# One decoder layer on one core: the key latent projected before the query latent, and the query latent's norm moved into the softmax

## The chip, the cores and the metric

The kernel runs on one core of one Trainium2 chip. The metric is the device time of one execution in microseconds. Engines are named as in the profile: PE (matrix multiply), PEld (its weight loads), DVE (VectorE), ACT (ScalarE), POOL (GpSimd), SP (SyncE, which issues most DMAs here).

## The reference, cut to what matters

The layer has 256 tokens, width 2048, and two attention groups of 8 heads that share one input projection. Group A is a dilated sliding-window attention. Group B is a multi-head latent attention: a 512-wide query latent and a 512-wide key/value latent are normalised, and projected up again to heads.

```python
a_q, a_k, a_v, c_q, c_kv, k_r = split(rmsnorm(x) @ w_in)
...                                        # group A
c_q = _rmsnorm(c_q, q_latent_norm)         # x * rsqrt(mean(x*x) + eps) * gain
q_b = c_q @ w_uq                           # 8 heads x (128 plain + 64 rotary)
q_rope = _rope(q_rope, positions)
c_kv = _rmsnorm(c_kv, kv_latent_norm)
kv = c_kv @ w_ukv                          # 8 heads x (128 key + 128 value)
k_rope = _rope(k_r, positions)             # one rotary key for all heads
b_out = softmax(causal(q_full @ k_full.T * (128 + 64) ** -0.5)) @ v_b
x = x + rmsnorm(concat(a_out, b_out) @ w_out)
x = x + rmsnorm(relu(rmsnorm(x) @ w_up) ** 2 @ w_down)
```

The query latent's reciprocal root mean square is one number for each token, and everything from the latent to the scores (projection, rotary, product with keys) is linear in it. It may therefore be multiplied in at the latent or at the scores of that query.

## The kernel before, in words

Every fp32 matrix product is done in three passes: each operand is split into a rounded part `hi` (ScalarE) and a rest `lo` (VectorE), and PE adds hi*hi, hi*lo and lo*hi in PSUM (`split`, line 310, and `split_gain`, line 316, which multiplies a gain in). Weights come by SP's DMA into five raw buffers (`Weights.load`, line 192), and are split into eight hi and eight lo buffers, six tiles ahead of their use (`Weights.emit` and `get`, lines 200 and 229). The order of the weight tiles is the order in which chunks are planned: lines 328 to 343. A tile is split only when the tile eight places earlier is used up.

The program is written out in one order for all engines, and every engine takes its own instructions of it in that order. A planner, `Flow` (line 135), decides the order while the program is traced. PE's projections are the main line and move a clock by the planner's own costs (`MM`, line 131, for a matmul of 512 columns; `TR`, line 132, for a transpose). Side work is written as generators ("chains") which yield a delay. After every few matmuls `pump` runs each chain whose time has come; `finish` runs chains until the named ones are done. The delays stand in lines 89 to 98. The clock is the planner's and not the chip's: where an engine is later than the planner thought, the engines behind it wait.

PSUM has eight banks. Four hold projections in turn (`acc_bank`, line 292), two hold transposes (`tp_bank`, line 295), two hold scores and attention outputs (`at_bank`, line 298). A group that takes a bank waits until the last reader of its former content is done.

The stretch around the change, after group A's projections:

- `proj` (line 463) of cq (line 749), then of ckv with the rotary key (line 752); ScalarE copies the results to SBUF, scaled by the first norm's rstd. Meanwhile group A's last four heads run as two chains (`heads_a`, line 653).
- `latent` (line 726) is a chain for each latent: ScalarE squares, VectorE and POOL make the rstd (`rstd_of`, line 499), VectorE multiplies it in (line 734), PE transposes in two groups (`cqt`, `ckvt`), and ScalarE and VectorE split each group into the transposed hi and lo with the latent's gain. The query's lies beside the ckv projection, the key's is started after it (line 776), and must be finished before k0 (line 851).
- `shared_key` (line 762): rotary on the 64 shared key columns, twice for the two halves of the partitions, two transposes (`krt`), two copies.
- The loop over `B_ORDER` (line 836): qr (rotary parts of all query heads), q0 and q1 (plain query heads 0 to 3 and 4 to 7), k0 and k1, v0 and v1. `columns` (line 785) makes heads with channels on partitions and asks for both weight tiles of its chunk at its start; `proj` makes tokens on partitions, and asks for one at a time. After qr the chain `query_ropes` (line 803) rotates and transposes (`qrt`).
- After k0, three workers (`heads_b`, line 817) take the heads w, w+3, w+6, started `D_PAIR` apart. Each waits, asking again every 0.5, until the chains of the rotary query and rotary key are gone and its keys are made; then scores (`sc_b`), softmax, transposes (`pT_b`), output (`o_b`), split into `mixT`.
- The output projection (`acc_o`) begins after v1, on group A's heads, and the last heads of B run among its matmuls.

Of the kernel before, what the change touches and what calls it, by code (L numbers as in the profile page):

```python
# [18 lines left out]
F32 = mybir.dt.float32  # L19
F32R = mybir.dt.float32r  # L20
I32 = mybir.dt.int32
BF16 = mybir.dt.bfloat16
AF = mybir.ActivationFunctionType
OP = mybir.AluOpType
PSUM = bass.MemoryType.PSUM

P = 128
D = 2048
S = 256
NB = S // P  # L30
KD = D // P
HA = 8
HB = 8
NOPE = 128
RB = 64
RA = 32
QR = 512
KVR = 512
# [5 lines left out]
SCALE_A = 128.0 ** -0.5  # L44
SCALE_B = float((NOPE + RB)) ** -0.5
# [35 lines left out]
X_PIECES = ((2, 1, 1), (3, 2, 2), (5, 4, 3), (8, 7, 3), (11, 10, 3), (14, 13, 3))  # L81

N_WARM = 8
B_ORDER = ("qr", "q0", "k0", "v0", "q1", "k1", "v1")
N_WORK = 3
OUT_PIECES = ((0, 0, 512), (1, 0, 512), (2, 0, 512), (3, 0, 256), (3, 256, 256))


DA = (3.0, 0.5, 3.0, 3.0, 4.0, 3.0, 0.5)
DB = (1.0, 0.5, 2.0, 3.0, 3.0, 2.0)  # L90
D_PAIR, D_KR = 3.5, 2.0
D_LOADED, D_LATENT = (13.0, 9.0), 3.5
D_X0, D_X, D_SS, D_TAB = 8.0, 3.0, 3.0, (14.0, 20.0)
D_NORM, D_HT, D_SECOND = 4.5, 1.5, 4.0

# [175 lines left out]
def layer(nc, tc, io):  # L271
    flow = Flow()
# [51 lines left out]
    weights = Weights(nc, wp, split, W_BUFS, W_AHEAD)  # L324
# [3 lines left out]
    w_in, K2 = io["w_in"], [2] * (KD // 2)  # L328
    ch_a = {}
    for half in range(2):  # L330
        if not half:
            ch_a[0, "qk"] = TwoChunk(weights, w_in, (0, 1024))
        for i, nm in enumerate("qkv"):
            if half or nm == "v":
                ch_a[half, nm] = Chunk(weights, w_in, i * 1024 + half * 512, 512, K2)
    ch_cq = Chunk(weights, w_in, 3 * 1024, QR, K2)
    ch_ckv = Chunk(weights, w_in, 3 * 1024 + QR, KVR + RB, [1] * KD, [(0, 288), (288, 288)])
    ch_b = []
    for what in B_ORDER:
        first = {"q": 0, "k": 0, "v": HB * NOPE}[what[0]] + 512 * (2 if what == "qr" else int(what[1]))  # L340
# [105 lines left out]
    for c in range(2):  # L446
        wide_d.append([])
        for what, k in DOWN_STEPS[c]:
            if what == "k":
                ts = [weights.plan(down_weight(c, k), 1, CW)]  # L450
            else:
                q, parts_q, back = [lambda c=c, k=k, f=f: f(c, k) for f in (down_sums, down_split, down_back)]
# [57 lines left out]
    pa = pool("pa", "right")  # L510
    early = pool("early", "left")
    mixT = [mix.tile([P, HA + HB, S], F32R, name=f"mixT_{w}") for w in ("hi", "lo")]
    mix.tile([P, 64], F32, name="mix_pad")
    xT = [pa.tile([P, KD, S], F32R, name=f"xT_{w}") for w in ("hi", "lo")]
# [42 lines left out]
    freq, bias_a, bias_b = cst[:, 0:192], cst[:, 192:448], cst[:, 448:704]  # L557
# [4 lines left out]
    rstd0 = []  # L562
# [56 lines left out]

    def softmax_pv(wk, dl, sc, bias, scale, v, head, name, need=lambda: True):  # L620

        s = wk.tile([P, 384], F32, tag="s", bufs=2 if scale == SCALE_A else N_WORK, name=f"s_{name}")
        st = wk.tile([P, 8], F32, tag="st", bufs=3, name=f"st_{name}")
        spans = ((0, 128, bias[:, 128:256]), (128, 384, bias))
        for i, (a, e, m) in enumerate(spans):
            nc.vector.tensor_tensor_reduce(
                out=s[:, a:e], in0=sc[:, a:e], in1=m, op0=OP.add, op1=OP.max, scale=1.0,
                scalar=-3e38, accum_out=st[:, i:i + 1])
        nc.vector.tensor_scalar_mul(st[:, 2:4], st[:, 0:2], -scale)
        yield dl[2]  # L630
        for i, (a, e, m) in enumerate(spans):
            nc.scalar.activation(s[:, a:e], s[:, a:e], AF.Exp, bias=st[:, 2 + i:3 + i], scale=scale,
                                 accum_out=st[:, 4 + i:5 + i])
        yield dl[3]
        nc.vector.reciprocal(st[:, 6:8], st[:, 4:6])
        for i, (a, e, m) in enumerate(spans):
            nc.vector.tensor_scalar_mul(s[:, a:e], s[:, a:e], st[:, 6 + i:7 + i])
        yield dl[4]
        tp = tp_bank(f"pT_{name}")
        for c in range(3):  # L640
            transpose(tp[:, c * P:(c + 1) * P], s[:, c * P:(c + 1) * P])
        pT = wk.tile([P, 384], F32, tag="pT", bufs=2 if scale == SCALE_A else N_WORK, name=f"pT_{name}")
        nc.scalar.activation(pT, tp[:, :384], AF.Copy)
        yield dl[5]
        while not need():
            yield 0.5
        o = at_bank(f"o_{name}")
        mm(o[:, :S], v[0], pT[:, :S], True, False, 2 * MM)
        mm(o[:, P:S], v[1], pT[:, S:384], False, True, MM)
        split(mixT[0][:, head, :], mixT[1][:, head, :], o[:, :S])  # L650
# [48 lines left out]
    heads, evacs = [], []  # L699
    for half in range(2):  # L700
        qkv = {}
        for nms in (("qk", "v") if not half else "qkv"):
            accs = [acc for _, _, acc in proj(xT, [ch_a[half, nms]], f"{nms}{half}",
                                              bank_of=at_bank if (half, nms) == (0, "v") else None)]
            for i, nm in enumerate(nms):
                if half and nm == "v":
                    flow.finish(*heads)
                if not half and nm != "v":
                    t = early.tile([P, NB + 1, 512], F32, name=f"{nm}_{half}")
# [10 lines left out]
    lat = pool("lat", "left")  # L720
    ckv = lat.tile([P, NB, KVR + RB], F32, name="ckv")
    cq = lat.tile([P, NB, QR], F32, tag="cq", name="cq")
    ss1 = con.tile([P, 2, NB], F32, name="ss1")
    latT = {"q": [t[:, HA + 4:, :] for t in mixT]}

    def latent(c, i, n, pl):

        for b in range(NB):
            junk = pl.tile([P, 512], BF16, tag="junk", bufs=1, name=f"junk_{n}{b}")
            nc.scalar.activation(junk, c[:, b, :512], AF.Square, accum_out=ss1[:, i, b:b + 1])  # L730
        rstd = rstd_of(ss1[:, i, :], NB, 512, n)
        yield 1.5
        for b in range(NB):
            nc.vector.tensor_scalar_mul(c[:, b, :512], c[:, b, :512], rstd[:, b:b + 1])
        yield 1.0
        cT = latT[n]
        for k2 in range(2):
            t = tp_bank(f"c{n}t_{k2}")
            for kk in range(2):
                k = 2 * k2 + kk  # L740
                for b in range(NB):
                    transpose(t[:, kk * S + b * P:kk * S + (b + 1) * P], c[:, b, k * P:(k + 1) * P])
            for kk in range(2):
                k = 2 * k2 + kk
                g = (4 if n == "kv" else 0) + k
                split_gain(cT[0][:, k, :], cT[1][:, k, :], t[:, kk * S:(kk + 1) * S], gcol[:, g:g + 1])
            yield 1.0

    for _, b, acc in proj(xT, [ch_cq], "cq"):
        nc.scalar.activation(cq[:, b, :], acc[0], AF.Copy, scale=rstd0[0][:, b:b + 1])  # L750
    q_chain = flow.start(latent(cq, 1, "q", lat), D_LATENT)
    for _, b, acc in proj(xT, [ch_ckv], "ckv"):
        for i in range(2):
            nc.scalar.activation(ckv[:, b, i * 288:(i + 1) * 288], acc[i][:, :288], AF.Copy, scale=rstd0[0][:, b:b + 1])
    flow.finish(q_chain, *heads)
    pa.release()
    pb = pool("pb", "right")


    krT = pb.tile([P, 2, S], F32, name="krT")  # L760

    def shared_key():
        kr = pb.tile([P, NB, 2, RB], F32, name="kr")
# [7 lines left out]
        for j in range(2):  # L771
            nc.vector.tensor_copy(krT[j * 64:(j + 1) * 64, j, :], t[j * 64:(j + 1) * 64, :S])

    latT["kv"] = [pb.tile([P, 4, S], F32R, name=f"ckvT_{w}") for w in ("hi", "lo")]
    pb.tile([P, 104], F32, name="pb_pad")
    kv_chain = flow.start(latent(ckv, 0, "kv", lat), 2.0)
    kr_chain = flow.start(shared_key(), D_KR)

    kT = pb.tile([P, HB, S], F32, name="kT")
# [37 lines left out]
    def heads_b(hs):  # L817
        for h in hs:
            while any(c in flow.chains for c in (qr_chain, kr_chain)):
                yield 0.5  # L820
            while f"k{h // 4}" not in made:
                yield 0.5
            yield DB[0]
            sc = at_bank(f"sc_b{h}")
            for o, b in ((0, 0), (128, 1)):
                n = (b + 1) * P
                qs = slice(b * P, (b + 1) * P)
                mm(sc[:, o:o + n], qT[:, h, qs], kT[:, h, :n], True, False, (b + 1) * MM)
                mm(sc[:, o:o + n], qrT[:, h // 2, qs], krT[:, h % 2, :n], False, True, (b + 1) * MM)
            yield DB[1]  # L830
            yield from softmax_pv(pb, DB, sc, bias_b, SCALE_B, [vB[:, b, h, :] for b in range(NB)], HA + h, f"b{h}",
                                  lambda: f"v{h // 4}" in made)
            made.add(h)

    workers = []
    for what, ch in ch_b:
        if what in ("qr", "v0", "v1"):
            if what == "qr":
                qr = lat.tile([P, NB, HB, RB], F32, tag="cq", name="qr")
            for _, b, acc in proj(latT["q" if what == "qr" else "kv"], [ch], what):  # L840
                if what == "qr":
                    out = qr[:, b].rearrange("p h d -> p (h d)")
                else:
                    i = 4 * int(what[1])
                    out = vB[:, b, i:i + 4, :].rearrange("p h d -> p (h d)")
                nc.scalar.activation(out, acc[0], AF.Copy)
            if what == "qr":
                qr_chain = flow.start(query_ropes(qr), 1.0)
        else:
            if what == "k0":  # L850
                flow.finish(kv_chain)
            t, i = qT if what[0] == "q" else kT, 4 * int(what[1])
            for h2, acc in columns(latT["q" if what[0] == "q" else "kv"], ch, what):
                h = i + 2 * h2
                nc.scalar.activation(t[:, h:h + 2, :].rearrange("p h s -> p (h s)"), acc, AF.Copy)
        made.add(what)
        if what == "k0":
            workers = [flow.start(heads_b(range(w, HB, N_WORK)), w * D_PAIR) for w in range(N_WORK)]


# [571 lines left out]
```

## Time and profile before

| what | value |
|---|---|
| three timed runs | 1034.48, 1035.3, 1038.92 us (median 1035.3) |
| profiled execution, whole | 1032.79 us |
| its span | 1031.0 us |
| granted PE clock | 0.998 |
| busy in the span: PE, DVE, ACT, POOL | 99%, 81%, 61%, 7% |
| cq projection | 144 to 170 us of the span |
| ckv projection | 170 to 200 us |
| qr to v1 | 200 to 259 us |
| output projection, up, down | 259 to 353, 353 to 690, 690 to 1023 us |

The span is the profiler's, from first to last instruction; the profiled execution's own time lies 1.8 us above it. A row of the timeline has its start, its busy time, engine, line, operation, output from inputs, count, and in brackets the idle time before it with what ended it. The line of a matmul is always the helper's (L303), so its tile's name tells what it belongs to; L313 and L314 are the plain split, L317 and L318 the split with a gain.

### The profile page before, as it was taken

The page shows a single profiled execution, that of the slowest core. Times are in us where ns is not written, and L with a number is a line of the kernel's source. Part 1 is how long each engine was busy: PE and PEld are TensorE (multiplying, and loading weights), DVE is VectorE, ACT ScalarE, POOL GpSimd, SP SyncE. Part 2 cuts the span into 40 slices and gives each one's busy share as a digit, 9 for nine tenths or more (in the row PEclk, how much of TensorE's full clock was granted, in tenths as well). Part 3 has the DMA queues.
Part 4 walks back from the last instruction along what each step waited for, and adds up shares of the span by engine and source line. Part 5 has one row for each costly group of instructions (what it writes and reads, how often), then busy time and mean ns, then how long its engine had stood idle before and what let it go on. Part 6 is the DMA issues. An engine that isn't in the chain of part 4 may idle for free.

```text
span 1031.0 us, 13295 instructions
## 1 busy us (share of the span) xinstructions
PE 1016.5 (99%) x4726; PEld 847.8 (82%) x4726; DVE 833.2 (81%) x1109; ACT 629.9 (61%) x838; POOL 73.7 (7%) x116
## 2 busy tenths in 40 slices
PE   9999999989999999999999999999999999999996
PEld 6888888989888878888888888888888888888885
DVE  6777655665547579999999999898999999898896
ACT  6675544645545467666775767666666665767571
POOL 0020100000001000000100100000101000211100
PEclk9999999999999999999999999999999999999999
DMA  9987553743466478877989878589989877889972
GB/s 297 370 258 248 191 196 99 245 151 105 145 221 188 138 299 279 271 244 253 284 257 303 277 246 266 189 267 349 350 265 366 299 239 262 297 310 304 318 262 82
DMA packets 106035, 257.65 MB, mean 250 GB/s; under 512 B 8944, under 2 KB 27888, under 8 KB 105584
## 3 DMA queue, kind: packets, MB, share of 16 engines
q1 hardware_dynamic: 65200, 175.14, 50.9%
q0 software_dynamic: 17392, 61.87, 18.1%
q10 hardware_dynamic: 23376, 19.78, 6.0%
q8 instruction: 37, 0.61, 0.2%
q14 instruction: 30, 0.25, 0.1%
HBM read 226.88 MB, written 29.89 MB: 249 GB/s over the span
## 4 chain that ended last, share of the span: by engine, by line
PE 79%; DVE 2%; issue 1%; DMA 1%; ACT 1%; POOL 0%; DVEq 0%; POOLq 0%; ACTq 0%
PE acc_u L303 26%; PE y L303 25%; PE acc_o L303 8%; PE md L303 6%; PE m L303 6%; PE acc_ckv L303 2%; PE acc_k L303 1%; PE acc_v L303 1%; PE sc_b L303 1%; PE acc_q L303 1%; DMA raw<-in_w_uq 1%; PE y L1300 1%; DVE lo L318 0%; PE o_b L303 0%; PE pT_b L307 0%
## 5 line engine op out<-in xcount | busy, mean ns | idle before, releaser
L314 DVE TENSOR_TENSOR lo<-raw,hi 128x1024 fp32r<-128x1024 f32 (+2 forms) x205 | 233.0, 1159 | 81.9 <-ACT hi L313 81.0
L313 ACT ACTIVATE hi<-raw 128x1024 fp32r<-128x1024 f32 (+2 forms) x205 | 202.1, 1004 | 76.7 <-DMA raw<-in_w_in 20.9
L303 PE MATMUL acc_u<-hi,hT_lo 128*128 128x512 f32 x386 | 150.3, 389 | 0.4 <-DVE hT_lo L314 0.4
L303 PE MATMUL acc_u<-hi,hT_hi 128*128 128x512 f32 x386 | 150.7, 390 | 0.0
L303 PE MATMUL acc_u<-lo,hT_hi 128*128 128x512 f32 x386 | 150.2, 389 | 0.0
L303 PE MATMUL y<-hi,uhi 128*128 128x512 f32 x358 | 139.3, 389 | 0.0
L303 PE MATMUL y<-lo,uhi 128*128 128x512 f32 x358 | 139.3, 389 | 0.0
L303 PE MATMUL y<-hi,ulo 128*128 128x512 f32 x358 | 139.3, 389 | 0.0
L317 ACT ACTIVATE hi<-raw,gcol 128x1024 fp32r<-128x1024 f32 x86 | 97.1, 1149 | 35.9 <-DMA raw<-in_w_up 15.4
L318 DVE SCALAR_TENSOR_TENSOR lo<-raw,gcol,hi 128x1024 fp32r<-128x1024 f32 x86 | 106.9, 1274 | 9.8 <-ACT hi L317 9.8
L303 PEld LDWEIGHTS acc_u<-hi,hT_lo 128*128 128x128 f32 x386 | 72.5, 188 | 16.0 <-DVE hT_lo L314 0.9
L303 PEld LDWEIGHTS acc_u<-hi,hT_hi 128*128 128x128 f32 x386 | 72.5, 188 | 14.8
L303 PEld LDWEIGHTS acc_u<-lo,hT_hi 128*128 128x128 f32 x386 | 72.5, 188 | 14.7
L303 PEld LDWEIGHTS y<-lo,uhi 128*128 128x128 f32 x358 | 67.2, 188 | 14.1
L303 PEld LDWEIGHTS y<-hi,uhi 128*128 128x128 f32 x358 | 67.2, 188 | 13.9
L303 PEld LDWEIGHTS y<-hi,ulo 128*128 128x128 f32 x358 | 67.2, 188 | 13.9
L314 DVE TENSOR_TENSOR lo<-st_down,hi 128x1024 fp32r<-128x1024 f32 x46 | 55.0, 1219 | 0.6 <-ACT hi L313 0.6
L303 PE MATMUL acc_o<-hi,mixT_hi 128*128 128x512 f32 x128 | 50.5, 394 | 0.0
L313 ACT ACTIVATE hi<-u 128x1024 fp32r<-128x1024 f32 (+1 forms) x33 | 32.2, 979 | 29.9 <-PE acc_u L303 12.8
L313 ACT ACTIVATE hi<-st_down 128x1024 fp32r<-128x1024 f32 x46 | 47.7, 1048 | 3.8 <-DVE st_down L370 2.4
L303 PE MATMUL md<-hi,s 128*128 128x512 f32 x138 | 49.9, 389 | 0.0
L303 PE MATMUL acc_o<-hi,mixT_lo 128*128 128x512 f32 x128 | 49.9, 390 | 0.0
(348 smaller groups left out, 2030.0 us busy)
## 6 DMA issues: line engine op xcount, KB each, us to landing
raw<-in_w_up SPq DMA_DIRECT2D x86, 512.0 KB, 4.9
raw<-in_w_down SPq DMA_DIRECT2D x82, 512.0 KB, 5.9
raw<-in_w_in SPq DMA_DIRECT2D x55, 512.0 KB, 5.7
ab<-in_w_up POOLq DMA_DIRECT2D x17, 1024.0 KB, 6.8
raw<-in_w_out SPq DMA_DIRECT2D x32, 512.0 KB, 4.7
ab_down<-in_w_down POOLq DMA_DIRECT2D x11, 1024.0 KB, 9.6
ulo<-ukeep POOLq DMA_DIRECT2D x20, 512.0 KB, 6.8
rkeep<-r ACTq DMA_DIRECT2D x28, 256.0 KB, 3.3
```

The lines of the kernel that those rows point to most:

```text
L303: nc.tensor.matmul(out, a, b, start=start, stop=stop)
L313: nc.scalar.activation(hi, src, AF.Copy)
L314: nc.vector.tensor_tensor(out=lo, in0=src, in1=hi.bitcast(F32), op=OP.subtract)
L317: nc.scalar.activation(hi, src, AF.Copy, scale=g)
L318: nc.vector.scalar_tensor_tensor(out=lo, in0=src, scalar=g, in1=hi.bitcast(F32), op0=OP.mult, op1=OP.subtract)
L1300: nc.tensor.matmul(out, a[x], w[z], start=False, stop=(x, z) == (1, 0), skip_group_check=True)
```

## The change

The key latent is projected first and the query latent second. The query latent is no longer multiplied by its rstd; the rstd, times the softmax scale and its negative, is kept in a small tile `by_query`, and the softmax takes it as a scale by partition (a partition is a query there). The chunks come as k0, qr, q0, v0, k1, q1, v1; the key latent's transposes take the place in `mixT` that the query's had, and the other way round. The workers start after q0, and ask for queries as well as keys. Some of the planner's delays change.

```diff
-B_ORDER = ("qr", "q0", "k0", "v0", "q1", "k1", "v1")
+B_ORDER = ("k0", "qr", "q0", "v0", "k1", "q1", "v1")
-D_PAIR, D_KR = 3.5, 2.0
-D_LOADED, D_LATENT = (13.0, 9.0), 3.5
+D_PAIR, D_KR = 3.5, 6.0
+D_LOADED, D_LATENT = (13.0, 9.0), 3.0
...
+    ch_ckv = Chunk(weights, w_in, 3 * 1024 + QR, KVR + RB, [1] * KD, [(0, 288), (288, 288)])
     ch_cq = Chunk(weights, w_in, 3 * 1024, QR, K2)
-    ch_ckv = Chunk(weights, w_in, 3 * 1024 + QR, KVR + RB, [1] * KD, [(0, 288), (288, 288)])
...
-        nc.vector.tensor_scalar_mul(st[:, 2:4], st[:, 0:2], -scale)
+        if isinstance(scale, float):
+            scales = [scale] * 2
+            nc.vector.tensor_scalar_mul(st[:, 2:4], st[:, 0:2], -scale)
+        else:
+            scales = [scale[:, 0, b:b + 1] for b in range(NB)]
+            nc.vector.tensor_tensor(out=st[:, 2:4], in0=st[:, 0:2], in1=scale[:, 1, :], op=OP.mult)
...
-            nc.scalar.activation(s[:, a:e], s[:, a:e], AF.Exp, bias=st[:, 2 + i:3 + i], scale=scale,
+            nc.scalar.activation(s[:, a:e], s[:, a:e], AF.Exp, bias=st[:, 2 + i:3 + i], scale=scales[i],
...
-    latT = {"q": [t[:, HA + 4:, :] for t in mixT]}
+    latT = {"kv": [t[:, HA + 4:, :] for t in mixT]}
...
         rstd = rstd_of(ss1[:, i, :], NB, 512, n)
-        yield 1.5
-        for b in range(NB):
-            nc.vector.tensor_scalar_mul(c[:, b, :512], c[:, b, :512], rstd[:, b:b + 1])
-        yield 1.0
+        if n == "kv":
+            yield 2.0
+            for b in range(NB):
+                nc.vector.tensor_scalar_mul(c[:, b, :512], c[:, b, :512], rstd[:, b:b + 1])
+            yield 3.0
+        else:
+            for j, f in enumerate((SCALE_B, -SCALE_B)):
+                nc.vector.tensor_scalar_mul(by_query[:, j], rstd, f)
...
-    for _, b, acc in proj(xT, [ch_cq], "cq"):
-        nc.scalar.activation(cq[:, b, :], acc[0], AF.Copy, scale=rstd0[0][:, b:b + 1])
-    q_chain = flow.start(latent(cq, 1, "q", lat), D_LATENT)
     for _, b, acc in proj(xT, [ch_ckv], "ckv"):
...
-    flow.finish(q_chain, *heads)
+    kv_chain = flow.start(latent(ckv, 0, "kv", lat), D_LATENT)
+    for _, b, acc in proj(xT, [ch_cq], "cq"):
+        nc.scalar.activation(cq[:, b, :], acc[0], AF.Copy, scale=rstd0[0][:, b:b + 1])
+    flow.finish(kv_chain, *heads)
...
+    by_query = pb.tile([P, 2, NB], F32, name="by_query")
...
-    latT["kv"] = [pb.tile([P, 4, S], F32R, name=f"ckvT_{w}") for w in ("hi", "lo")]
+    latT["q"] = [pb.tile([P, 4, S], F32R, name=f"cqT_{w}") for w in ("hi", "lo")]
...
-    kv_chain = flow.start(latent(ckv, 0, "kv", lat), 2.0)
+    q_chain = flow.start(latent(cq, 1, "q", lat), 2.0)
...
-            while f"k{h // 4}" not in made:
+            while not {f"k{h // 4}", f"q{h // 4}"} <= made:
...
     for what, ch in ch_b:
+        if what == "qr":
+            flow.finish(q_chain)
...
-            if what == "k0":
-                flow.finish(kv_chain)
...
-        if what == "k0":
+        if what == "q0":
             workers = [flow.start(heads_b(range(w, HB, N_WORK)), w * D_PAIR) for w in range(N_WORK)]
```

More of the change, by code (lines that the diff above doesn't have):

```diff
@@ L620, in softmax_pv @@
     def softmax_pv(wk, dl, sc, bias, scale, v, head, name, need=lambda: True):
-        s = wk.tile([P, 384], F32, tag="s", bufs=2 if scale == SCALE_A else N_WORK, name=f"s_{name}")
+        s = wk.tile([P, 384], F32, tag="s", bufs=2 if wk is pa else N_WORK, name=f"s_{name}")
         st = wk.tile([P, 8], F32, tag="st", bufs=3, name=f"st_{name}")
@@ L641, in softmax_pv @@
             transpose(tp[:, c * P:(c + 1) * P], s[:, c * P:(c + 1) * P])
-        pT = wk.tile([P, 384], F32, tag="pT", bufs=2 if scale == SCALE_A else N_WORK, name=f"pT_{name}")
+        pT = wk.tile([P, 384], F32, tag="pT", bufs=2 if wk is pa else N_WORK, name=f"pT_{name}")
         nc.scalar.activation(pT, tp[:, :384], AF.Copy)
@@ L830, in heads_b @@
             yield DB[1]
-            yield from softmax_pv(pb, DB, sc, bias_b, SCALE_B, [vB[:, b, h, :] for b in range(NB)], HA + h, f"b{h}",
+            yield from softmax_pv(pb, DB, sc, bias_b, by_query, [vB[:, b, h, :] for b in range(NB)], HA + h, f"b{h}",
                                   lambda: f"v{h // 4}" in made)
```

## The prediction

> **What bounds the kernel now.** I began with the page's first part: the PE is busy for all but 14.5 us of the span, so an edit can take time away only where the PE stands still, or add it by making it stand still.
>
> ```profile
> span 1031.0 us, 13295 instructions
> PE 1016.5 (99%) x4726; PEld 847.8 (82%) x4726; DVE 833.2 (81%) x1109; ACT 629.9 (61%) x838; POOL 73.7 (7%) x116
> ```
>
> The table of waits, for the PE alone, then says where. Four of its waits lie in the stretch that the diff touches: for the transposes of the two latents (cqt, ckvt) and for one score.
>
> ```profile
> PE ckvt L307 <- DVE ckvT_lo L318: 2.6, 1, 2.6
> ...
> PE cqt L307 <- DVE mixT_lo L318: 1.1, 1, 1.1
> PE ckvt L307 <- DVE ckv L734: 0.5, 1, 0.5
> ...
> PE sc_b L303 <- DVE mixT_lo L314: 0.3, 1, 0.3
> ```
>
> The busy time by stretch (columns: PE, PEld, DVE, ACT, POOL, clock, DMA share, GB/s) agrees, and shows that what follows has no hole in the PE.
>
> ```profile
> 170.00:200.00 30.00, 28.86 (x215) 28.27 (x214) 20.29 (x37) 19.95 (x40) 0.72 (x1) 1.00 0.61 187
> 200.00:230.00 30.00, 26.95 (x178) 24.44 (x177) 21.30 (x41) 16.93 (x30) 1.17 (x2) 1.00 0.55 179
> ...
> 370.00:690.00 320.00, 320.00 (x1414) 265.05 (x1413) 295.26 (x341) 217.61 (x253) 20.22 (x26) 1.00 0.82 269
> ```
>
> A wait costs more than its idle time, because the end of a matmul is modelled. In the PE's timeline starts of ckv matmuls lie 0.13 apart, so the second cqt group came 181.59 - 180.22 - 0.13 = 1.24 late, 0.16 more than its 1.08.
>
> ```profile
> 180.22 0.29 PE L303 MATMUL acc_ckv<-hi,xT_lo 128*128 128x288 f32 x1
> 181.59 0.63 PE L307 MATMUL cqt<-ident,cq 128*128 128x128 f32 x4 [1.08 <-DVE mixT_lo L318]
> ...
> 265.55 1.47 PE L303 MATMUL o_b<-pT_b,vB 128*128 128x256 f32 x8
> 267.30 0.49 PE L303 MATMUL sc_b<-kT,qT 128*128 128x128 f32 x2 [0.28 <-DVE mixT_lo L314]
> ```
>
> With 0.16 added to each, the four waits cost 4.5 + 0.64 = 5.1 us. That is all there is to win here.
>
> **What goes.** The old order starts the key latent's chain when the PE has only qr and q0 left to run, and transposes the key latent, the shared key and the key latent again through two PSUM banks in turn; the third group waits for the bank of the first, which VectorE leaves late, having weight splits ahead. In the new order the key latent has the whole cq projection as cover. I followed the planner's clock by hand with its own costs (lines 89 to 98, 131, 132), first for the kernel before, where it gives the order of the trace, then for the diff. Between the two ckvt groups of the new order no other transpose is issued (both second heads of A have theirs before them), and between the two cqt groups neither, since the shared key is due at 6.0. So each pair takes both banks. The 1.1 + 2.6 + 0.5 go, and the score's 0.3 passes into the waits of third outputs, below. Gain 5.1. The two 128x512 scalings of cq also go from VectorE; they lay beside PE work and are worth nothing. The matmuls and weight bytes are the same, and SP still loads in the order of use; only the 16 ckv and 8 cq tiles, and the pairs of w_uq and w_ukv, change places.
>
> **What comes.** Prices of groups on the PE come from the chain of waits.
>
> ```profile
> 178.95 0.45 PE cqt L307 x4
> ...
> 212.28 4.31 PE acc_q L303 x36
> ...
> 225.29 1.31 PE sc_b L303 x8
> ...
> 232.10 1.31 PE sc_b L303 x8
> ...
> 237.00 0.33 PE pT_b L307 x3
> ...
> 248.40 2.07 PE acc_v L303 x9
> ...
> 255.52 0.65 PE o_b L303 x4
> ```
>
> First the query latent. Let the PE leave cq at time 0. It runs k0 (48 matmuls at 4.31/36 = 0.12, so 5.75) with both cqt groups among it (0.87), reaches qr at 6.6, and after 15 of its matmuls (0.23 each) the shared key's transposes at 10.0. Against it run these, from the timelines of the PE, ScalarE, VectorE and GpSimd:
>
> ```profile
> 238.59 0.28 PE L303 MATMUL acc_k<-ckvT_hi,hi 128*128 128x256 f32 x1
> 238.79 0.60 ACT L855 ACTIVATE qT<-acc_q 128x512 f32<-128x512 f32 x1 [0.78 <-PE acc_q L303]
> 239.29 2.00 ACT L313 ACTIVATE hi<-raw 128x1024 fp32r<-128x1024 f32 x2
> 240.37 2.36 DVE L314 TENSOR_TENSOR lo<-raw,hi 128x1024 fp32r<-128x1024 f32 x2 [2.28 <-ACT hi L313]
> ...
> 202.00 0.62 ACT L730 ACTIVATE junk_kv<-ckv 128x512 bf16<-128x512 f32 x1
> 203.28 0.19 ACT L730 ACTIVATION_READ_ACCUMULATOR junk_kv<-ckv 128x1 f32 x1
> 203.75 0.70 POOL L505 TENSOR_TENSOR rstd_kv<-t_kv,neg_half 128x2 f32<-128x2 f32 x1 [26.93 <-DVE t_kv L504]
> 203.61 0.29 DVE L615 TENSOR_TENSOR rp_kr<-ckv,trig 128x128 f32<-128x128 f32 x1
> 205.31 0.29 DVE L618 TENSOR_TENSOR kr<-rp_kr,rp_kr 128x128 f32<-128x128 f32 x1
> 210.51 0.47 ACT L317 ACTIVATE ckvT_hi<-ckvt,gcol 128x256 fp32r<-128x256 f32 x1 [1.51 <-DVE ckvT_lo L318]
> 211.02 0.48 DVE L318 SCALAR_TENSOR_TENSOR ckvT_lo<-ckvt,gcol,ckvT_hi 128x256 fp32r<-128x256 f32 x1 [0.54 <-ACT ckvT_hi L317]
> ```
>
> A copy out of PSUM starts 0.2 after the PE moves on (238.59 to 238.79). So ScalarE copies cq by 0.9, splits both v0 tiles (k0 is a column chunk and asks for both) by 2.8, and squares (1.47, from 202.00 to 203.47) by 4.25; the rstd's small VectorE step and POOL's 0.70 take it to 5.2. Now the diff's new wait: the two by_query products stand in VectorE's queue right behind, and the latent's lo halves behind them. I take 0.2 for each product, near the small steps between 203.47 and 203.75, so 5.6. Then hi and lo alternate at about 0.5 a piece in one bank: lo 0 at 6.1, lo 1 at 7.1, lo 2 at 7.6, lo 3 at 8.6. The qr matmuls need lo 0 at 7.1 and lo 1 at 7.75: they fit, by 0.65 at the tightest. The eight rotary steps of the shared key (203.61 to 205.6, 2.0) come next, done at 10.65, and its transposes, due on the PE at 10.0, wait 0.7. Bounds: 0 if VectorE is 0.7 earlier, 2.0 if the ropes begin a whole rope length late.
>
> Second the heads of B, where most of the loss is. Before, the query's rotary chain was finished when the three workers began, so their scores stayed 3.4 apart (225.29 to 232.10 for three). Now qr comes after k0, and its chain is due 1 + 4 + 4 + 1 + 1 = 11 after qr ends, while the workers start after q0 (48 x 0.114 = 5.5 on the planner's clock) at 5.5, 9.0 and 12.5. The first two poll every 0.5 until the chain is gone, at about 12, and the third arrives then: all three scores are issued in one go, and so are the heads 3 to 5 after them. Three heads share two score banks and two transpose banks, so each third group waits for the first one's reader. Rows of the timelines and of the groups for 140 to 290:
>
> ```profile
> 236.04 0.16 DVE L635 RECIPROCAL st_b<-st_b 128x2 f32<-128x2 f32 x1
> ...
> 236.69 0.15 DVE L635 RECIPROCAL st_b<-st_b 128x2 f32<-128x2 f32 x1
> ...
> 256.49 0.39 ACT L632 ACTIVATE s_b<-s_b,st_b 128x128 f32<-128x128 f32 x1
> ...
> 257.37 0.39 ACT L632 ACTIVATE s_b<-s_b,st_b 128x128 f32<-128x128 f32 x1
> ...
> L643 ACT ACTIVATE pT_b<-pT_b 128x384 f32<-128x384 f32 x8 | 3.8, 490 | 10.5 <-PE pT_b L307 10.5
> L846 ACT ACTIVATE vB<-acc_v 128x512 f32<-128x512 f32 x4 | 2.4, 594 | 2.4 <-PE acc_v L303 2.3
> ...
> L750 ACT ACTIVATE cq<-acc_cq,rstd_pre 128x512 f32<-128x512 f32 x2 | 1.4, 680 | 1.0 <-PE acc_cq L303 1.0
> ```
>
> - Scores 0, 1, 2 begin 24 matmuls (2.9) into k1, and the third is wanted 2.6 later, at 5.5. VectorE has two lo splits ahead, to 4.1 (as 238.59 to 242.7), then the maxima of score 0, which ends at 4.2: about 0.9, an estimate from 0.29 for the 128x128 step at 203.61 and twice the columns beside it. It fits, by 0.4. Cost 0.
> - Transposes 0, 1, 2 come 0.7 after q1 ends. The first one's copy stands behind q1's copy and a weight split on ScalarE (free at 1.7: 239.29 and half of 2.00, less 238.59), takes 0.49, so the third starts at 2.2 instead of 1.35: 0.85.
> - Outputs 0, 1, 2: a bank came free 267.30 - 266.20 = 1.1 after o_b ended (265.55 + 0.65), and one other o_b covers 0.65 of it: 0.45. Outputs 3, 4, 5 the same: 0.45.
> - Transposes 3, 4, 5 come 42 matmuls of 0.23 (9.55) after the last score. ScalarE's queue holds v1's first copy (to 2.85), three heads' exponentials (0.88 each from 256.49 to 257.37, and 0.09 more per activation for a scale read from memory, as 680 against 594; to 6.0), v1's second copy and a split, to 7.6. VectorE's lo half (1.2) and three normalisations (0.65 each, 236.04 to 236.69) end at 10.8 where 10.2 was wanted: 0.7 with the copy's wait.
>
> New waits 0.7 + 0.85 + 0.9 + 0.7 = 3.15; bounds 0.9 (the two output waits alone, which have a direct row) and about 7 (every one of the seven groups a whole microsecond). The longer exponentials are on the path only in that last item; elsewhere ScalarE's idle share hides their 1.5 us. Softmax's own product replaces one small VectorE step by another.
>
> **Sum.** 3.15 - 5.1 = -1.95, say -1.8, as cq's first matmul may wait 0.15 for a bank. The profiled execution took 1032.8 for its span of 1031.0, and comes out at 1031.0. The three runs shown have a median of 1035.3, 2.5 above it; I forecast against that: 1033.5.
>
> [...]
>
> **Rivals.**
> - Bunching costs little. The chain by query is 0.7 faster, and the transposes find ScalarE free; only the output waits stay. -5.1 + 0.9 = -4.2: 1031.1. For it: ScalarE is 56% busy there. Against: copies behind weight splits at 239.29.
> - The query latent comes late (the slower side). The place is qr's first matmuls, the price one for one beyond 0.65 of lateness; from 0.65 + 1.8 = 2.45 late the kernel is no faster. If the second v0 tile were still in flight for a landing of 5.5 when ScalarE asks, 4.85 is lost: +3.0, 1038.3. For it: ScalarE did wait for such a tile, 1.11. Against: five raw buffers of 2.7 us of PE work each run ahead in cq.
>
> ```profile
> 198.02 1.06 ACT L313 ACTIVATE hi<-raw 128x1024 fp32r<-128x1024 f32 x1 [1.11 <-DMA raw<-in_w_ukv]
> ...
> raw<-in_w_ukv SPq DMA_DIRECT2D x8, 512.0 KB, 5.5
> ```
>
> - Eaten later: VectorE is 92% busy from 370 to 690. 1035.3. Against: no PE wait there.
> - It doesn't do what it says: a transpose of A falls between the ckvt groups after all and the old 1.24 stays. 1034.7.
>
> **Numbers.** Chances: forecast 0.50 (its own range 1031.5 to 1035), little cost 0.20, late latent 0.13, eaten 0.09, wait stays 0.08. About 0.5% (5.2 us) is what a measurement of this kernel can tell from no change. Faster by that needs all of the 5.1 and luck: half of the second case and a little, 0.13. Slower by it needs the late latent beyond its priced size: 0.08. Same 0.79. The bounds of the new waits, 0.9 and 7, give 1031.1 and 1037.2; the range adds 1.6 below, as the runs shown differ by more, and most of the late latent's case above: 1029.5 to 1037.5.
>
> **What would show it.** Right: no PE wait at cqt or ckvt; three sc_b groups back to back, twice; short PE waits at krt, at the third pT_b (for ScalarE's copy) and third o_b (for mixT_lo). Wrong: scores still 3.4 apart; a PE wait at acc_qr; a new wait after 370; DMA waits on ScalarE around 195 to 205.

## The result and the profile after

The changed kernel took 1030.38 us in the median of six runs (1029.56 to 1031.63), the kernel before 1035.2 beside it (six runs, 1034.48 to 1038.92). The ratio is 0.9947, with a 95% interval of 0.9931 to 0.9964: about 5 us faster, and not clearly more or less than 0.5%. Timed once more against other runs of the kernel before (`after_again`, below), the ratio was 0.9963 (0.9949 to 0.9976). The forecast was 1033.5: the direction was right and the measured time lies inside the range, but the gain was more than twice the 1.8 forecast.

The profiled execution has a span of 1028.7 us, 2.3 below that of before. The first rows of its page show the same matmuls as before, 4726, and PE idle for 11.5 us where it was 14.5.

```profile
span 1028.7 us, 13299 instructions
...
PE 1017.2 (99%) x4726; PEld 848.3 (82%) x4726; DVE 832.2 (81%) x1109; ACT 631.3 (61%) x838; POOL 73.4 (7%) x116
```

The table of PE's waits after the change (engine, line, what released it, us in total, times, longest) has no row for cqt, ckvt, krt or acc_qr. What is new are the third transposes and outputs of B's heads.

```profile
PE pT_b L307 <- ACT pT_b L648: 0.6, 1, 0.6
PE o_b L303 <- DVE mixT_lo L314: 0.6, 2, 0.3
PE acc_u L303 <- DVE hT_lo L314: 0.4, 1, 0.4
```

The stretch between the first matmul of the first latent and the first of acc_u holds all that the diff touches. Its ends are the first starts of these rows (times of one, then first and last start in us), first of the kernel before, then of the changed one.

```profile
L303 PE MATMUL acc_cq<-hi,xT_hi x32: 389/389/579, 144.0 to 168.5; 128*128 128x512 f32 x32
...
L303 PE MATMUL acc_u<-hi,hT_hi x386: 387/389/482, 352.7 to 689.5; 128*128 128x512 f32 x193
```

```profile
L303 PE MATMUL acc_ckv<-hi,xT_hi x64: 288/296/485, 144.1 to 173.8; 128*128 128x288 f32 x64
...
L303 PE MATMUL acc_u<-hi,hT_hi x386: 387/389/487, 349.5 to 686.4; 128*128 128x512 f32 x193
```

That is 352.7 - 144.0 = 208.7 before and 349.5 - 144.1 = 205.4 after: the stretch became 3.3 shorter. The same boundaries for every profile of this study (us; the labels are those of the experiments below):

| profile | span | this stretch | first acc_u to first y | first y to PE's last matmul |
|---|---|---|---|---|
| before | 1031.0 | 208.7 | 337.5 | 332.3 |
| before_look1 | 1034.8 | 210.2 | 337.5 | 334.1 |
| before_look2 | 1032.8 | 208.8 | 337.5 | 334.7 |
| e3_unscaled_alone | 1032.3 | 208.8 | 337.5 | 334.1 |
| e4_shared_key_late | 1034.3 | 209.5 | 337.6 | 334.3 |
| e5_kept_busy | 1033.1 | 208.7 | 338.8 | 332.9 |
| after | 1028.7 | 205.4 | 337.6 | 333.1 |
| after_look1 | 1030.4 | 205.4 | 337.6 | 334.8 |
| after_again | 1028.1 | 205.4 | 337.7 | 332.3 |
| e1_staggered | 1026.4 | 203.2 | 337.5 | 333.8 |
| e2_query_scaled | 1030.8 | 207.5 | 337.5 | 333.0 |

Two things are to be seen. The changed stretch repeats to 0.1 us in all three profiles of the new kernel, so its 3.3 is no accident of one execution. And the last stage, which the diff doesn't touch, moves between 332.3 and 334.8 in either kernel. PE waits there for split weights, in two looks as follows (before_look2, then after_look1), and in the first profile of before not at all. The prediction was built on that profile, whose last stage is the shortest of its order by chance; this is why the two spans differ by 2.3 only.

```profile
PE y L303 <- DVE lo L314: 1.6, 1, 1.6
```

```profile
PE y L303 <- DVE lo L314: 1.9, 2, 1.1
```

The planner's order came out as predicted by hand. In the chain of the changed kernel (start, us, what) both ckvt groups stand among the cq matmuls without a wait, both cqt groups among those of k0, and the scores of three heads come in one block of 24 matmuls, twice.

```profile
184.65 0.44 PE ckvt L307 x4
...
185.80 0.44 PE ckvt L307 x4
...
201.36 0.44 PE cqt L307 x4
...
202.51 0.44 PE cqt L307 x4
...
226.60 3.93 PE sc_b L303 x24
...
241.18 0.55 PE pT_b L307 x3
...
244.71 0.92 PE o_b L303 x4
245.63 3.93 PE sc_b L303 x24
```

### The profile page after: what moved, and what is told of

It reads as the page before. It is cut to its first block, busy times and chain, and to the rows that moved or that the text cites. A ratio compares the mean times of both kernels' runs of the same rounds, so it can differ in the third digit from the quotient of the medians.

```text
span 1028.7 us, 13299 instructions
## 1 busy us (share of the span) xinstructions
PE 1017.2 (99%) x4726; PEld 848.3 (82%) x4726; DVE 832.2 (81%) x1109; ACT 631.3 (61%) x838; POOL 73.4 (7%) x116
## 4 chain that ended last, share of the span: by engine, by line
PE 85%; DMA 6%; DVE 4%; ACT 2%; issue 2%; POOL 0%; SPq 0%; DVEq 0%; POOLq 0%; ACTq 0%
PE acc_u L303 26%; PE y L303 23%; PE acc_o L303 8%; PE m L303 6%; PE md L303 5%; DMA raw<-in_w_in 4%; PE acc_k L303 3%; PE acc_v L303 3%; PE acc_ckv L303 2%; PE acc_cq L303 2%; PE acc_q L303 2%; DVE lo L314 2%; DMA ab_down<-in_w_down 1%; ACT hi L313 1%; PE sc_b L303 1%
## 5 line engine op out<-in xcount | busy, mean ns | idle before, releaser
L313 ACT ACTIVATE hi<-u 128x1024 fp32r<-128x1024 f32 (+1 forms) x33 | 32.2, 979 | 30.2 <-PE y L303 11.5
```

The source lines that it names most:

```text
L313: nc.scalar.activation(hi, src, AF.Copy)
```

## Experiments

### e1_staggered: the changed kernel, with the heads of B set apart again

```diff
         yield 0.5
+    if h < N_WORK:
+        yield h * D_PAIR
     yield DB[0]
```

> The changed kernel, with its three workers set apart again: each waits h * D_PAIR more ahead of its first score. By my theory the changed kernel pays about 2 us for three heads in one go (third pT_b and third o_b, twice): these waits go, and the time is 1028.4, 2 below the changed kernel's 1030.4. By the rival, that the bunched heads cost nothing that is not given back later, it stays at 1030.4. Above 1031 both are wrong.

Measured: 1028.91 us, ratio to the kernel before 0.9936 (0.9918 to 0.9954), stretch 203.2. From the first latent on, PE has only these two waits, both outside the stretch:

```profile
PE y L303 <- DVE lo L314: 0.8, 1, 0.8
PE acc_u L303 <- DVE hT_lo L314: 0.4, 1, 0.4
```

Its chain shows why: three scores lie 4.2 and 3.5 apart, with projection between them, and no transpose or output waits for a bank.

```profile
225.87 1.31 PE sc_b L303 x8
...
230.05 1.31 PE sc_b L303 x8
...
233.51 1.31 PE sc_b L303 x8
```

What follows: the bunched heads cost 205.4 - 203.2 = 2.2 us, and what there was to win is 208.7 - 203.2 = 5.5. The rival that bunching costs next to nothing beyond the output waits falls. This version is also the quickest that was run.

### e2_query_scaled: the changed kernel, with the query latent multiplied by its rstd

```diff
-        if n == "kv":
+        if n == "q":
+            yield 1.5
+            for b in range(NB):
+                nc.vector.tensor_scalar_mul(c[:, b, :512], c[:, b, :512], rstd[:, b:b + 1])
+            yield 1.0
+        else:
...
-            yield from softmax_pv(pb, DB, sc, bias_b, by_query, ...
+            yield from softmax_pv(pb, DB, sc, bias_b, SCALE_B, ...
```

> The changed kernel, with the query latent multiplied by its rstd in place again (as the kernel before does) and the softmax with its constant scale; order and delays of the changed kernel otherwise. By my theory the transposes then wait for squares, rstd and scaling, with only k0 as cover: PE waits of 1.1 at cqt and about 1.5 at qr, some 3 in all, so 1033.4. By the rival, that the gain is the order alone and the unscaled latent gives nothing, 1030.4.

Measured: 1032.89 us, ratio 0.9976 (0.9962 to 0.9990), stretch 207.5, which is 2.1 above the changed kernel. The table of PE's waits has one new row in it, the shared key's, and none at cqt or qr, where the waits were expected:

```profile
PE pT_b L307 <- ACT pT_b L648: 1.0, 2, 0.7
PE krt L307 <- DVE kr L618: 0.6, 1, 0.6
```

PE's timeline has the expected waits all the same, inside groups that the table doesn't take apart:

```profile
204.86 0.28 PE L303 MATMUL acc_k<-mixT_hi,lo 128*128 128x256 f32 x1
205.24 1.28 PE L307 MATMUL cqt<-ident,cq 128*128 128x128 f32 x8
206.65 0.50 PE L303 MATMUL acc_qr<-hi,cqT_hi 128*128 128x512 f32 x1
...
209.01 0.40 PE L303 MATMUL acc_qr<-hi,cqT_lo 128*128 128x512 f32 x1
210.00 0.41 PE L307 MATMUL krt<-ident,kr 128*128 128x128 f32 x2 [0.60 <-DVE kr L618]
```

What follows: in the new place, the unscaled query latent is worth 2.1 us, together with the two delays that the scaling brings. From the first matmul of k0 to the first of q0, PE takes 14.45 us here (199.23 to 213.68) and 12.42 in the changed kernel (199.04 to 211.46): 2.03 of the 2.1. Both cqt groups now stand behind k0 in one row. From its last matmul to the first of qr pass 1.79, where one matmul (0.12) and two groups (0.36 each, as in the changed kernel) make 0.84. From there to krt pass 3.35, where nine matmuls at 0.23 make 2.07. So about 1 us is lost at cqt and some 1.2 at qr and krt: the waits were expected in the right places, though the one at krt was not named, and 3 us was too much. The two waits at pT_b are not new: the changed kernel has the second of them as well, hidden in a merged row (the third pT_b of heads 3 to 5, further down).

### e3_unscaled_alone: the kernel before, with the unscaled query alone

```diff
-        for b in range(NB):
-            nc.vector.tensor_scalar_mul(c[:, b, :512], c[:, b, :512], rstd[:, b:b + 1])
+        if n == "kv":
+            ...                                  # as before
+        else:
+            for j, f in enumerate((SCALE_B, -SCALE_B)):
+                nc.vector.tensor_scalar_mul(by_query[:, j], rstd, f)
...
-            yield from softmax_pv(pb, DB, sc, bias_b, SCALE_B, ...
+            yield from softmax_pv(pb, DB, sc, bias_b, by_query, ...
```

> The kernel before with the unscaled query latent alone (rstd in the softmax, delays and order as before). By my theory the two scalings lay beside PE work and the rstd is not on its path: 1035.2, within 1. By the rival, that the scaling was itself the cause of the late transposes, the wait at the second cqt group goes with it: 1034.0 or less.

Measured: 1035.46 us, ratio 1.0003 (0.9983 to 1.0023), stretch 208.8. The old waits are all there:

```profile
PE ckvt L307 <- DVE ckvT_lo L318: 2.5, 1, 2.5
PE cqt L307 <- DVE mixT_lo L318: 1.1, 1, 1.1
...
PE ckvt L307 <- DVE ckv L741: 0.5, 1, 0.5
```

What follows: in the old order the scalings lay beside PE work and were worth nothing, as the prediction said. The gain is the new order's; the unscaled query is what keeps the new order from a new wait.

### e4_shared_key_late: the kernel before, with the shared key's chain started later

```diff
-D_PAIR, D_KR = 3.5, 2.0
+D_PAIR, D_KR = 3.5, 6.0
```

> The kernel before with the shared key's delay alone changed from 2 to 6, so that its transposes no longer stand between the two groups of the key latent. By my theory the second ckvt group then has the other bank, its wait of 2.7 goes and no more than 0.5 comes in its place at k0: about 1032.8. By the rival, that the wait is VectorE's lateness and not the bank, the same microseconds turn up at k0: 1035.2.

Measured: 1036.08 us, ratio 1.0005 (0.9992 to 1.0018), stretch 209.5. The saving did not come. No ckvt group waits, but the shared key's transposes stand still as long in their place:

```profile
213.76 0.41 PE L307 MATMUL krt<-ident,kr 128*128 128x128 f32 x2 [2.75 <-issue]
```

The delay starts the whole chain of the shared key later, its rotary steps too. In the kernel before VectorE does them from 203.61 to 205.60 (rows in the prediction). Here they stand behind two weight splits and two of the latent's lo halves, and the last ends at 213.65:

```profile
208.16 2.36 DVE L314 TENSOR_TENSOR lo<-raw,hi 128x1024 fp32r<-128x1024 f32 x2 [1.24 <-ACT hi L313]
...
211.86 0.28 DVE L615 TENSOR_TENSOR rp_kr<-ckv,trig 128x128 f32<-128x128 f32 x1
...
213.36 0.29 DVE L618 TENSOR_TENSOR kr<-rp_kr,rp_kr 128x128 f32<-128x128 f32 x1
```

What follows: the prediction put the 2.6 before ckvt down to the bank that the shared key shares with it. With the bank free the wait at ckvt is gone, as this explanation asks for, and it did not turn up at k0 either. But the edit moves VectorE's rotary steps along with the bank, and they bring a wait of the same size to krt. So the run does not show what the free bank alone would be worth. The changed kernel has neither wait: it gives the latent's work the cq projection as cover as well as two banks, and no run tells the two apart.

### Looks at the two kernels, and a clock that falls

> The kernel before, unchanged, for another profile. The timed median moved by 4.8 us, while the two profiled executions differ by 2.3. By my theory the changed stretch (from the first matmul of the latents' projections to the first acc_u) takes the same 208.7 in every execution of this kernel, and what varies lies after 690 us, where the first profile had a lucky 340.8 to its end and most executions take 1 to 2 more. By the rival the stretch itself is longer in most executions (210 or more), and its first profile was lucky there.

> The changed kernel, unchanged, for another profile. By my theory the changed stretch takes 205.4 again, within 0.3, and the stretch from the first y to the end varies as in the kernel before (341 to 343). By the rival the changed kernel is also shorter after 690 us, below 341.

> As the other look at the kernel before: by my theory 208.7 in the changed stretch, 341 to 343 from the first y to the end; by the rival 210 or more in the changed stretch.

Measured: 1036.52, 1032.14 and 1034.61 us; stretches 210.2, 205.4 and 208.8, and a last stage of 334.1, 334.8 and 334.7. The last stage does move in either kernel. The 210.2 was not expected; it is the rival's number, in one of three profiles of the kernel before. Busy time in windows of 4 us (columns as in the prediction, the clock after POOL's) shows where it is from: in this execution of the kernel before, the granted clock falls right after the wait at ckvt, to 0.65 and then 0.93. The rows of before_look1:

```profile
208.00:212.00 4.00, 1.50 (x12) 1.27 (x11) 3.32 (x5) 1.89 (x4) 0.00 (x0) 1.00 0.68 228
212.00:216.00 4.00, 3.93 (x23) 3.96 (x24) 3.37 (x8) 1.13 (x3) 0.00 (x0) 0.65 0.49 165
216.00:220.00 4.00, 4.00 (x33) 4.00 (x32) 2.30 (x5) 1.77 (x4) 0.00 (x0) 0.93 0.00 0
```

The first profile of before, with the same wait, kept its clock and ran 36 matmuls in the window where this one ran 23:

```profile
212.00:216.00 4.00, 4.00 (x36) 4.00 (x35) 3.38 (x8) 1.44 (x3) 0.00 (x0) 1.00 0.43 154
```

In before_look1's timeline of PE the q0 matmuls start 0.12 apart, then about 0.215 apart from 213.28 to 216.49, then 0.12 again:

```profile
212.89 0.28 PE L303 MATMUL acc_q<-mixT_hi,hi 128*128 128x256 f32 x1
213.01 0.28 PE L303 MATMUL acc_q<-mixT_lo,hi 128*128 128x256 f32 x1
...
213.50 0.41 PE L303 MATMUL acc_q<-mixT_lo,hi 128*128 128x256 f32 x1
213.72 0.41 PE L303 MATMUL acc_q<-mixT_hi,lo 128*128 128x256 f32 x1
```

At 0.215 a piece, 3.2 us hold 15 matmuls, which cost 15 x 0.095 = 1.4 more than at 0.12: the 1.5 by which this stretch is above 208.7. The run e4 shows the same after its wait of 2.75 (0.84 and 0.73 from 212 to 220), so that its 209.5 would by estimate be about 208 without it, 0.7 below the kernel before. A granted clock of 0.65 and 0.93 in two windows of 4 us lacks (0.35 + 0.07) x 4 = 1.7 us of full clock. Over the 3.2 us of wide starts this is by estimate a clock of about 0.5; at just half speed it would fill 3.4 us. The fall comes here after 2.57 us of idle time, with 0.48 and short bursts of work ahead of it. The first profile of before has 2.58 and 0.47 at the same places, and no fall: the same idle time is not followed by it in every execution.

### e5_kept_busy: the kernel before, with PE kept at work in its wait

The twelve added products are read by nobody; all else is computed as before.

```diff
         for k2 in range(2):
+            if n == "kv" and k2:
+                for w in range(2):
+                    spare = at_bank(f"spare{w}")
+                    for _ in range(6):
+                        nc.tensor.matmul(spare[:, :P], ident, ident, start=True, stop=True)
             t = tp_bank(f"c{n}t_{k2}")
```

> The kernel before, with twelve 128x128 matmuls of the identity into two idle banks put on TensorE just ahead of the second four transposes of the key latent, where it waits 2.6 us; their result is read by nobody, and everything else stands in its old order. What is open: in one look at the kernel before, and in the run with the shared key late, the granted clock fell after this wait to 0.65 and 0.93 (212 to 220 us), and to 0.84 and 0.73, and the stretch from the first latent matmul to the first acc_u was 210.2 us where three other profiles of that order (the kernel before twice, the unscaled query alone) had 208.7 to 208.8. Theory (the wait is followed by a stretch of some 3.4 us at half clock in about half of the executions, because TensorE is idle in it: 14 of 29 executions of the kernel before show a mean clock of 0.996 or less, 0 of 13 of the changed one and the one with the staggered heads): the idle time before these transposes falls from 2.6 to under 0.7, the stretch stays at 208.7 (the transposes still start when VectorE is done), no more than 1 execution in 10 shows a mean clock of 0.996 or less, and the median is 0.8 (half of 1.7) below that of the kernel before. Rival (the low clock comes from the chip and not from the wait): the share of low clocks stays near one half and the median within 0.3 of the kernel before.

> The changed kernel once more, timed beside the kernel before and the one kept busy. Theory: stretch 205.4 us, no clock of 0.996 or less, and a median 4.1 below the kernel before (3.3 of waits and 0.8 of clock), 3.3 below the one kept busy. Rival: 4.1 below both, since keeping TensorE busy gains nothing.

Measured: e5 1035.19 us, ratio 0.9997 (0.9987 to 1.0008); the changed kernel 1031.01, ratio 0.9963 (0.9949 to 0.9976). In e5 PE is busy where it stood still (compare the rows above), and of the two ckvt waits only the short one is left:

```profile
208.00:212.00 4.00, 4.00 (x37) 3.95 (x36) 3.45 (x5) 1.64 (x3) 0.00 (x0) 1.00 0.70 229
```

```profile
PE ckvt L307 <- DVE ckv L734: 0.5, 1, 0.5
```

The mean granted clock of each execution, counted over all runs:

| kernel | executions | of these at 0.996 or less |
|---|---|---|
| before, beside e1 to e4 | 29 | 14 |
| before, beside e5 | 18 | 11 |
| e3_unscaled_alone | 12 | 5 |
| e4_shared_key_late | 12 | 9 |
| e5_kept_busy | 12 | 0 |
| changed kernel (all runs), e1_staggered and e2_query_scaled | 32 | 2 |

The count is a rough measure: the 1.7 us of clock that before_look1 lacks in its two windows lower the mean over 1031 us by 0.0016, near the rounding of these figures, and the profile of e4, which shows the fall (0.84 and 0.73), has a mean of 0.997.

What follows: in these counts the low clock goes with the idle PE. It is found in 14 of 29, 11 of 18, 5 of 12 and 9 of 12 executions of the kernels that have the long wait (2.5 to 2.8 us), and in none of 12 when PE is given the twelve products to do in it. What it is worth in the median stays open. In the first four rows the executions at the low clock have medians 0.3, 1.1, 1.2 and 2.5 us above the others of the same row. But e5 came out 0.26 above the kernel before and not 0.8 below, and the changed kernel 3.9 below the kernel before and 4.2 below e5, which is the rival's forecast (4.1 below both). The expected 0.8 us would be a ratio of 0.9992, which the interval holds, as it holds 1. The one profile of e5 has the 208.7 expected, and lost 1.2 elsewhere, at a wait for split weights in the up projection (338.8 in the table), which no other profile has there.

## Why the prediction was right in direction and short in size

Its terms, against what the profiles of before, of the changed kernel and of e1 show for each (us):

| step of the prediction | predicted | measured |
|---|---|---|
| waits at cqt, ckvt and the score removed | -5.1 | -5.5 (e1 against before) |
| wait at krt | +0.7 | 0 |
| third pT_b, heads 0 to 2 | +0.85 | +0.81 (0.65 idle and 0.16) |
| third o_b, both times | +0.9 | +0.88 (0.28 + 0.16, twice) |
| third pT_b, heads 3 to 5 | +0.7 | +0.47 |
| bank at cq's start | +0.15 | 0 |
| sum | -1.8 | -3.3 |

**The removed waits** were read short by 0.3, and the reason stands in the trace of before. The first ckvt group and the second do the same work, but from the start of the group to that of the next instruction the first takes 207.97 - 207.28 = 0.69 and the second 212.03 - 211.65 = 0.38. The first stops inside itself, between two of its four transposes, which a view by groups doesn't list. 4.5 + 0.64 + 0.31 is the 5.5 that e1 recovers.

```profile
207.28 0.85 PE L307 MATMUL ckvt<-ident,ckv 128*128 128x128 f32 x4 [0.47 <-DVE ckv L734]
207.97 0.38 PE L307 MATMUL krt<-ident,kr 128*128 128x128 f32 x2
...
211.65 0.63 PE L307 MATMUL ckvt<-ident,ckv 128*128 128x128 f32 x4 [2.58 <-DVE ckvT_lo L318]
212.03 0.36 PE L303 MATMUL acc_q<-mixT_hi,hi 128*128 128x256 f32 x1
```

**The wait at krt** is the term that failed. The prediction had VectorE done with the rotary steps 10.65 after PE leaves cq, and PE there at 10.0. PE left cq at 199.04 and reached krt at 209.13, 10.1 later: right. VectorE was done at 208.69 + 0.29 = 208.98, 9.9 later, which leaves 0.15 to spare. Its rows in the changed kernel:

```profile
204.20 0.47 DVE L744 TENSOR_SCALAR by_query<-rstd_q 128x2 f32<-128x2 f32 x2 [0.80 <-POOL rstd_q L505]
204.34 0.48 DVE L318 SCALAR_TENSOR_TENSOR cqT_lo<-cqt,gcol,cqT_hi 128x256 fp32r<-128x256 f32 x1
...
206.78 0.48 DVE L318 SCALAR_TENSOR_TENSOR cqT_lo<-cqt,gcol,cqT_hi 128x256 fp32r<-128x256 f32 x1 [0.54 <-ACT cqT_hi L317]
207.19 0.28 DVE L615 TENSOR_TENSOR rp_kr<-ckv,trig 128x128 f32<-128x128 f32 x1
...
208.69 0.29 DVE L618 TENSOR_TENSOR kr<-rp_kr,rp_kr 128x128 f32<-128x128 f32 x1
```

The first lo half starts 0.14 after the first of the two by_query products, although these are busy for 0.47: neighbours on VectorE overlap here, and the prediction laid them end to end (5.6 for the end of the products and 8.6 for the end of the lo halves, where the trace has the first lo half start at 5.3 and the rotary steps begin at 8.15). The rotary steps took 1.8 and not 2.0. A margin of 0.15 is thin, as e2 shows: with the scalings ahead and the cqt groups later, krt waits 0.6. The prediction's "0 if VectorE is 0.7 earlier" named the bound that came true.

**The bunched heads** were priced rightly, 2.45 against 2.2, with the waits at the places named. The forecast of what releases them was right for heads 0 to 2 (ScalarE's copy, from 240.64, behind a weight split of 1.05 from 239.70) and for the outputs (mixT_lo). For heads 3 to 5 it named VectorE's normalisations; the chain has ScalarE's copy instead, the third group starting at 260.08, 1.13 after the first at 258.95, where three groups of 0.33 would have it at 0.66. In PE's timeline the three are one row, so no wait is listed. VectorE's last normalisations (259.57 and 0.55 busy) end hardly sooner, so that term was close in size.

```profile
258.95 1.68 PE L307 MATMUL pT_b<-ident,s_b 128*128 128x128 f32 x9
```

```profile
259.54 0.50 ACT pT_b L648
260.08 0.55 PE pT_b L307 x3
```

**The rest.** qr's matmuls fit, as said, and so did the scores; no DMA holds ScalarE in the new order (its waits from 170 to 230 list none, where the kernel before has 1.1 at raw<-in_w_ukv). The explanation of the old 2.6 by the shared bank fits e4, where the wait at ckvt goes with it; what the bank alone is worth stays open, since e4 moves VectorE's work too, and the new order gives both the banks and VectorE their time. Beyond the sum, the forecast took the median of three runs as its base and the wait as its only price. The timed kernels differ by 4.8 in the medians of the first comparison and 3.9 in those of the second, where the stretch gives 3.3: the low clock, in 25 of 47 executions of the kernel with the old wait, points the right way, but was not shown to fill that gap.

**The rivals.** "Bunching costs little" names 1031.1, the time nearest to the result, for a wrong reason: bunching cost 2.2, and the time came from krt and from the longer removed waits. "The query latent comes late" did not happen, but e2 has a mild form of it. "Eaten later" fell: the 3.3 are still there at PE's last matmul, since the stage from acc_u to y is as long in both kernels and the last one moves by its own chance. PE's idle time told the gain of this edit, 5.5 with e1. That the wait stays fell too.

## What to carry to other kernels

When a wait ends at a semaphore of a shared buffer, free that buffer and nothing else to test it: the delay that freed the bank here moved VectorE's work as well, and a wait of the same size (2.75 for 2.58) came up at the next group. In the changed kernel, with more work between the producer and the need as well, neither wait is left. When side chains are polled for one common event, see whether they leave together: here they did (24 score matmuls in one block, twice), and the two-deep buffer rotations behind them paid at each third member (0.81, 0.44 twice and 0.47); a stagger put after the event, not before it, gave back 2.2 us. And price neighbours on one engine by their start-to-start distance, and groups of PE by the distance to the next instruction: here busy times overlapped (0.47 busy, the next start 0.14 later) and a wait hid inside a group (0.69 where the same work took 0.38).

## What was not expected of the hardware

A wait of 2.6 us on PE was followed by 3.2 us in which matmuls started 0.215 apart in place of 0.12, at a granted clock of 0.65 and 0.93 in the two windows of 4 us, in one of three profiles of the kernel before. By the mean clock, about half of its executions are low (25 of 47 at 0.996 or less, 0 of 12 with PE kept busy). In that profile the changed stretch was 1.5 us longer than in the other two (210.2 against 208.7 and 208.8), so one profile may not show what a wait costs.

The last stage waits for split weights for 0 to 1.9 us, differently in each execution of either kernel. A single pair of profiles can be off by 2 us for this alone: the first pair had 2.3 between its spans and 3.3 between its changed stretches.
